# One remainder modulo 256 bytes for every operand of a matrix product: SBUF layout of a hybrid decoder block

## The chip, the cores and the metric

The kernel runs on one core of a Trainium2 chip. The metric is device time in microseconds (us): 2110.35 us is the median of three runs of the kernel before (2109.66 to 2110.6).

## The reference

One decoder block on a sequence of 2048 tokens, width 1024, all in float32. Cut to what matters:

```python
def reference(x, p, w_in, ...):            # x (1, 2048, 1024), p (1, 1, 2048, 256)
    xn = rmsnorm(h, pre_gain)
    z = xn @ w_in                          # (2048, 6152): q, k, v, f logits, g_attn, x_lru, g_lru
    q, k, v, fl, g_attn, x_lru, g_lru = split(z)
    o_attn = forgetting_attention(q, k, v, fl + b_f)      # causal, 8 heads of 128
    y_attn = rmsnorm(o_attn, attn_out_gain) * silu(g_attn)
    xc = causal_depthwise_conv(x_lru, conv_w, conv_b)     # width 4
    o_lru = rg_lru(xc, ...)                # two 128x128 gate products a block, then a scan
    y_lru = rmsnorm(o_lru, lru_out_gain) * silu(g_lru)
    mix = concat([y_attn, y_lru]) @ w_out  # (2048, 2048) @ (2048, 1024)
    h = h + rmsnorm(mix, post_gain)
    e = rmsnorm(p @ w_ple, ple_gain)       # (2048, 256) @ (256, 1024)
    gate = sigmoid(h @ w_ple_gate + b_ple_gate)
    return h + gate * e
```

## The kernel before

Every large product is made of float32r pieces: an operand is split into a high part and the rest (`split`), and `mm3` issues three products (lines 66, 67, 68: high x high, and the two mixed ones) into one PSUM bank. On top of that, the products with `w_in` and `w_out` use seven block products instead of eight (Strassen-Winograd), with sums of blocks formed by VectorE, GpSimd and ScalarE.

The program has three stages in time. **Projections** (to about 1068 us): `z = xn @ w_in`, in two passes over halves of the tokens. Work is divided into units: `v` (v columns and the forget logits, 258 columns wide), `l` (LRU input and gate), `k` (k and q), `g` (attention gate). Every unit has seven block products, `i` = 0 to 6; a unit other than `v` issues 12 products of 128x512 for each `i`, with tokens `XH[i]`, `XL[i]` as the moving operand (512 columns) and a weight block as the stationary one (128x128). For `v` it is the other way round. **Attention** (about 1068 to 1600 us): scores `sbank`, transposes of the probabilities with the identity matrix `ident` (`tbank`), values `obank`. **Output** (to the end): the product with `w_out` (`pbank<-wa,xh` and the like), and the gate product with `w_ple_gate` (`pbank<-wg,h`).

The order of the projections is written out by hand: `plan(slot, phase, f)` puts a step into a calendar of slots (one slot is one block product, 12 matrix products), and the steps are issued slot by slot, in each slot by phase: LOAD, COMBINE, PREP, JOB, MUL, GATE, STORE. All loads and stores of this stage are issued on the SP queue, in calendar order; a load into a tile of a ring waits there until the tile's last user is done, and what follows it on SP waits too. `Ring` computes from the ring's size when a tile comes free.

In the first pass `load_raw` loads a unit's four raw weight quadrants, one to a tile `wf` (ring of 8); `sums`, `high` and `low` make from them the seven operands in tiles `op` (ring of 5: high part in the first half, rest in the second); `keep` stores each to DRAM. In the second pass `fetch` brings the operands back: of nine fetches, five go whole into an `op` tile and four go into two `wf` tiles, one for each part (names `wh`, `wl`).

A tile takes its place in SBUF from its pool's order and size. `wf` tiles have 516 elements (2064 bytes, placed 2080 bytes apart), `op` tiles 2 x 516 (4128 bytes). So operands of one product lie at different remainders modulo 256 bytes. From the built program, remainder modulo 256 of the address at which a partition's data begins:

| tiles | before | after |
|---|---|---|
| `XH`, `XL` of i = 0, 5, 1, 2 | 224 | 224 |
| `XH`, `XL` of i = 3, 4, 6 | 192 | 224 |
| the five `op` slots | 224, 0, 32, 64, 96 | 224 in each |
| `wh`, `wl` (`wf` slots; after: `wr` in `wq` slots) | 224, 0, 32, ... 192 | 224 in each |
| `wph`, `ph` (embedding product) | 192, 64 | 224, 224 |
| LRU gates `xch`, `wgh` | 96, 96 (first pass), 224, 224 | 224, 224 |
| `kh`, `vh` (even, odd heads) | 224, 64 | 224, 224 |
| `qh`, `th`, `tl` | 96 | 224 |
| `ident`; `pr` | 0; 224, 96 | 224; 224, 224 |
| output stage `wa`, `wb`, `xh`, `wg`, `h` | 160, all alike | 224, all alike |

Steps of 512 bytes inside a tile do not change the remainder. In `v` units the moving operand starts at multiples of 1032 bytes, so it has 224, 232, 240 or 248 after.

Of the kernel before, what the change touches and what calls it, by code (L numbers as in the profile page):

```python
# [16 lines left out]
P = 128  # L17
# [15 lines left out]
WS = 2 * WV  # L33
NOP = 5
NOPB = 4
# [36 lines left out]
def hymba_kernel(ctx: ExitStack, tc: tile.TileContext, x, xT, pT, w_p, w_v, w_o, w_ple, w_pg,  # L72
# [27 lines left out]
    ident = const.tile([P, P], F32, name="ident")  # L100
    make_identity(nc, ident)
    onesq = const.tile([P, P], F32, name="onesq")
    nc.gpsimd.memset(onesq, 1.0)
    cmask = const.tile([P, P], F32, name="cmask")
    nc.gpsimd.memset(cmask, 0.0)
    nc.gpsimd.affine_select(out=cmask, in_=cmask, pattern=[[-1, P]], compare_op=ALU.is_ge,
                            fill=-1.0e30, base=0, channel_multiplier=1)
# [13 lines left out]
    rstd_e = const.tile([P, TB], F32, name="rstd_e")  # L121

# [109 lines left out]

    op_ring, wf_ring, ws_ring = Ring(NOP), Ring(8), Ring(2)

    class Unit:
# [17 lines left out]
        def load_raw(self, quad, hf):  # L253
            f = wp.tile([P, WS], F32, name="wf", bufs=8)
            src = w_v[self.n, quad, :, hf * WS:(hf + 1) * WS] if self.v else w_p[self.n, quad]
            nc.sync.dma_start(out=f[:, :self.cols], in_=src)
            self.raw[quad, hf] = f

        def raws(self, hf):
            n = self.cols  # L260
            return [self.raw[q, hf][:, :n] if (q, hf) in self.raw else None for q in range(4)]

        def sums(self, i, hf):
            n = self.cols
            a11, a12, a21, a22 = self.raws(hf)
            sub = lambda o, x, y: nc.gpsimd.tensor_tensor(out=o, in0=x, in1=y, op=ALU.subtract)
            if i == 1 and self.v or i == 2 and not self.v:
                self.S[1, hf] = wp.tile([P, WS], F32, name="ws", bufs=2)[:, :n]
                nc.gpsimd.tensor_tensor(out=self.S[1, hf], in0=a21, in1=a22, op=ALU.add)
            if i == 2:  # L270
                self.S[2, hf] = self.S[1, hf] if self.v else wp.tile([P, WS], F32, name="ws", bufs=2)[:, :n]
# [25 lines left out]
        def fetch(self, i, hf, whole):  # L297
            n = self.cols
            if whole:
                op = wp.tile([P, 2 * WS], F32R, name="op", bufs=NOP)  # L300
                nc.sync.dma_start(out=f32(op[:, :2 * n]), in_=self.stored(i, hf))
                self.ops[i, hf] = op[:, :n], op[:, n:2 * n], op
            else:
                hi = wp.tile([P, WS], F32R, name="wh", tag="wf", bufs=8)
                lo = wp.tile([P, WS], F32R, name="wl", tag="wf", bufs=8)
                nc.sync.dma_start(out=f32(hi[:, :n]), in_=self.stored(i, hf)[:, :n])
                nc.sync.dma_start(out=f32(lo[:, :n]), in_=self.stored(i, hf)[:, n:2 * n])
                self.ops[i, hf] = hi[:, :n], lo[:, :n], None

    def plan_weights(u, lead=4):  # L310

        ends, starts = {}, {}
        halves = range(u.halves)
        quads_of = {0: (0,), 5: (1,), 1: (2, 3), 2: (0, 2, 3), 3: (1,), 4: (0, 2), 6: (3,)}
        for i in u.prep:
            for hf in halves:
                end = u.use(i) + u.halves - 1
                s = max(op_ring.free(), u.use(i) - lead)
                if i == (1 if u.v else 2):
                    s = max(s, ws_ring.ends[-1] + 2 if ws_ring.ends else s)  # L320
                op_ring.take(s, end)
                if u.use(i) - s < 2:
                    print("late operand", u.kind, u.h, i, hf, u.use(i) - s)
                starts[i, hf] = s
                if i in (1, 2, 3, 4):
                    plan(s - 1, PREP, lambda i=i, hf=hf: u.sums(i, hf))
                plan(s, PREP, lambda i=i, hf=hf: u.high(i, hf))
                plan(s + 1, COMBINE, lambda i=i, hf=hf: u.low(i, hf))
                plan(min(s + 2, end), STORE, lambda i=i, hf=hf: u.keep(i, hf))
            if i == 3:  # L330
                ws_ring.take(s, s + 1)
        for quad in (0, 1, 2, 3):
            for hf in halves:
                users = [starts[i, hf] - (i in (1, 2, 3, 4)) for i in u.prep if quad in quads_of[i]]
                last = max(starts[i, hf] + (1 if i in (0, 5, 6) or (i, quad) == (4, 2) else -1)
                           for i in u.prep if quad in quads_of[i])
                s = max(wf_ring.free(), min(users) - lead)
                wf_ring.take(s, last)
                if min(users) - s < 2:
                    print("late raw", u.kind, u.h, quad, hf, min(users) - s)  # L340
                plan(s, LOAD, lambda quad=quad, hf=hf: u.load_raw(quad, hf))
# [3 lines left out]
    def plan_fetch(u):  # L345

        for i in u.order:
            for hf in range(u.halves):
                end = u.use(i) + u.halves - 1
                whole = fetched[0] % (NOP + NOPB) >= NOPB  # L350
                fetched[0] += 1
                ring = op_ring if whole else wf_ring
                s = max(ring.free(), u.use(i) - 7)
                ring.take(s, end)
                if not whole:
                    s = max(s, ring.free())
                    ring.take(s, end)
                if u.use(i) - s < 3:
                    print("late fetch", u.kind, u.h, i, hf, u.use(i) - s)
                plan(s, LOAD, lambda i=i, hf=hf, whole=whole: u.fetch(i, hf, whole))  # L360
# [82 lines left out]
    def plan_v(u, vp):  # L443
# [23 lines left out]
        def combine(i, t):  # L467
            new = {0: "u1", 1: "u5", 5: "o11", 3: "o12"}.get(i)
            if new and t == 0:
                T[new] = vp[0].tile([P, 4, WV], F32, name=names[new], bufs=1)  # L470
# [39 lines left out]
    def plan_job(lw, hb, c, t, new_head):  # L510
# [9 lines left out]
        def s0():  # L520
            J.X = tile_("X", 2, n=515)
# [102 lines left out]
    sg, vp, lw, s = [None], [None], [None, None], {}  # L624
    right = {}

    def open_right(name, cell):
        right[name] = ctx.enter_context(ExitStack())
        cell[0] = pool_(right[name], name, side="right")

# [7 lines left out]
    def square(n, kk, engs):  # L638

        src = s[n, kk // 4][:, kk % 4]  # L640
        eng = engs[kk]
        if (n, eng) not in acc_x:
            acc_x[n, eng] = sg[0].tile([P, 512], F32, name="rx", bufs=2 + len(set(engs)) - 1)
            nc.scalar.activation(acc_x[n, eng], src, AF.Square)
            return
        t = ctile()
        nc.scalar.activation(t, src, AF.Square)

        def accumulate():
            (nc.vector if eng == "dve" else nc.gpsimd).tensor_tensor(out=acc_x[n, eng], in0=acc_x[n, eng], in1=t,  # L650
                                                                     op=ALU.add)
        plan(now[0] + 1, COMBINE, accumulate)

    def column_sums(n):
        accs = [acc_x.pop(k) for k in list(acc_x) if k[0] == n]
        b = er_x[n] = sbank()
        for i in range(4):
            for m, a in enumerate(accs):
                nc.tensor.matmul(b[:, i:i + 1], lhsT=a[:, i * P:(i + 1) * P], rhs=onesq[:, 0:1],
                                 start=m == 0, stop=m == len(accs) - 1)  # L660
# [13 lines left out]
    def spread_scales(n):  # L674
        r_x[n] = sbank()
        nc.tensor.matmul(r_x[n], lhsT=onesq, rhs=dg_x.pop(n), start=True, stop=True)
# [36 lines left out]
    ess = te.tile([P, TB, 2], F32, name="ess", bufs=1)  # L713
# [11 lines left out]
    def ple_weight(j, k):  # L725
        js = slice(j * 512, (j + 1) * 512)
        wf = E["w", j, k] = wp.tile([P, WS], F32, name="wf", bufs=8)[:, :512]
# [20 lines left out]
    def embed_out(tb):  # L748
        b2 = E.pop(("b", tb))
        for j in range(2):  # L750
            js = slice(j * 512, (j + 1) * 512)
            if tb < 4:
                if j == 0:
                    E["v"] = vp[0].tile([P, 4, WV], F32, name=("u1", "u5", "o11", "o12")[tb], bufs=1)
                eo = E["o", tb, j] = E["v"].rearrange("p a b -> p (a b)")[:, js]
# [4 lines left out]
    def embed_sum():  # L760
        nc.vector.tensor_tensor(out=rstd_e, in0=ess[:, :, 0], in1=ess[:, :, 1], op=ALU.add)
# [9 lines left out]
    open_right("sgA", sg)  # L771
# [29 lines left out]
    for n, when in enumerate(((1, 1, 1, 2, 2, 2, 3, 3), (4, 4, 4, 5, 5, 5, 6, 6))):  # L801
        for kk in range(8):
            plan(when[kk], JOB, lambda n=n, kk=kk: square(n, kk, ["dve"] * 8))
# [31 lines left out]
    for _ in range(4):  # L835
        wf_ring.take(-4, -2)
# [64 lines left out]
    plan(130, LOAD, lambda: open_right("sgB", sg))  # L901
    for n in range(2):
# [3 lines left out]
        for kk in range(8):  # L906
            plan(134 + 5 * n + kk // 2, JOB, lambda n=n, kk=kk: square(n, kk, ["dve"] * 8))
# [31 lines left out]
    def bias_tiles():  # L939
        B_.a, B_.b, B_.mg = (vp[0].tile([P, 4, WV], F32, name=x, bufs=1).rearrange("p a b -> p (a b)")  # L940
                             for x in ("u1", "u5", "o11"))
# [120 lines left out]
    def first_mask_adds():  # L1062
        u0.r4 = kvA_[0].tile([P, 4], F32, name="r4", bufs=1)
# [148 lines left out]
    def score_units(h, g, u):  # L1212
# [4 lines left out]
        u.r4 = av.tile([P, 4], F32, name="r4", bufs=4)  # L1217
# [341 lines left out]
    sa = w1.tile([P, TB], F32, name="sa")  # L1559
# [353 lines left out]
```

## Time and profile before

| what | value |
|---|---|
| median of three runs | 2110.35 us (2109.66 to 2110.6) |
| profiled execution: its time, its span | 2115.7 us, 2113.6 us |
| granted TensorE clock | 0.996 |
| TensorE (PE) busy | 2084.5 us, 99% of the span |
| VectorE (DVE), ScalarE (ACT), GpSimd (POOL) busy | 77%, 54%, 33% |
| DMA | 518.91 MB, mean 246 GB/s |

Reading it: PE is the TensorE row; a busy PE does not say that its products run as fast as they can. In groups of instructions ("line engine op, out<-in, shape xcount | busy us, mean ns") the mean of a product counts from its start to its modelled end, and products overlap: the distance from one start to the next is what fills the time. Lines 66, 67 and 68 are the three products of `mm3`; the tile names tell the stage.

### The profile page before, as it was taken

Reading aid. Unit: us, or ns where it says so; the run is one execution under the profiler, and the core shown is the slowest. Engines: PE = TensorE matmul, PEld = TensorE weight load, DVE = VectorE, ACT = ScalarE, POOL = GpSimd, SP = SyncE. Lnnn points to the kernel's source line nnn. Section 1 sums busy time; section 2 is a strip of 40 time slices with the busy share of each in tenths; the row PEclk is TensorE's granted clock in tenths of the full one; section 3 lists DMA queues with packets and bytes.
Section 4 is the critical chain, followed back from the end, with each engine's and each line's share of the span. In section 5 each row is a group of like instructions: output and inputs, shape, how many; then the busy total and the mean of one; then the engine's idle time right before and its main releaser. Section 6 shows DMA issues by size and latency. Waiting matters only on the chain.

```text
span 2113.6 us, 31607 instructions
## 1 busy us (share of the span) xinstructions
PE 2084.5 (99%) x10586; PEld 1743.1 (82%) x10586; DVE 1630.3 (77%) x2706; ACT 1145.6 (54%) x1871; POOL 705.4 (33%) x612
## 2 busy tenths in 40 slices
PE   8899999999999999999999999999999999999999
PEld 6788888888988888888878888888887888888887
DVE  7977988696758877886578888888884778776665
ACT  6435755444337776664267776777674444442232
POOL 3534455332203334733015655566552000000000
PEclk9999999999999999999999999999999999999999
DMA  8598898988888889887757767777653887665553
GB/s 310 204 326 288 296 346 309 341 311 300 286 274 267 281 252 302 267 286 252 267 174 225 231 208 224 232 226 235 200 163 115 278 258 230 194 215 174 180 174 120
DMA packets 274834, 518.91 MB, mean 246 GB/s; under 512 B 27104, under 2 KB 93936, under 8 KB 274672
## 3 DMA queue, kind: packets, MB, share of 16 engines
q1 hardware_dynamic: 274528, 516.86, 74.4%
q8 instruction: 83, 1.36, 0.3%
q14 instruction: 79, 0.65, 0.1%
q10 hardware_dynamic: 144, 0.05, 0.0%
HBM read 314.55 MB, written 202.25 MB: 245 GB/s over the span
## 4 chain that ended last, share of the span: by engine, by line
PE 91%; DVE 4%; DMA 2%; ACT 1%; issue 1%; SPq 0%; POOL 0%; DVEq 0%; ACTq 0%
PE bank L67 15%; PE bank L68 15%; PE bank L66 15%; PE pbank L66 7%; PE pbank L68 7%; PE pbank L67 7%; PE tbank L1261 5%; PE sbank L66 3%; PE sbank L68 3%; PE sbank L67 3%; PE obank L67 3%; PE obank L68 3%; PE obank L66 2%; PE bank L1783 1%; PE tbank L1280 1%
## 5 line engine op out<-in xcount | busy, mean ns | idle before, releaser
L66 PE MATMUL bank<-XH,op 128*128 128x512 f32 x876 | 347.2, 396 | 0.0
L67 PE MATMUL bank<-XL,op 128*128 128x512 f32 x876 | 345.9, 395 | 0.0
L68 PE MATMUL bank<-XH,op 128*128 128x512 f32 x876 | 345.7, 395 | 0.0
L363 DVE TENSOR_TENSOR c<-bank,c 128x512 f32<-128x512 f32 x280 | 186.7, 683 | 125.5 <-PE bank L68 118.1
L58 DVE TENSOR_TENSOR tl<-tbank,th 128x512 fp32r<-128x512 f32 (+1 forms) x320 | 192.2, 607 | 83.9 <-ACT th L52 79.9
L52 ACT ACTIVATE th<-tbank 128x512 fp32r<-128x512 f32 (+1 forms) x320 | 167.6, 530 | 118.2 <-PE tbank L1261 110.4
L68 PEld LDWEIGHTS bank<-XH,op 128*128 128x128 f32 x876 | 164.7, 188 | 39.3
L66 PEld LDWEIGHTS bank<-XH,op 128*128 128x128 f32 x876 | 164.6, 188 | 39.2 <-issue 0.5
L67 PEld LDWEIGHTS bank<-XL,op 128*128 128x128 f32 x876 | 164.7, 188 | 39.1 <-issue 0.5
L1234 ACT ACTIVATE pr<-pr,m 128x640 f32<-128x640 f32 (+7 forms) x124 | 151.9, 1225 | 44.9 <-DVE m L1225 44.5
L1261 PE MATMUL tbank<-ident,pr 128*128 128x128 f32 x1088 | 171.9, 273 | 0.0
L1261 PEld LDWEIGHTS tbank<-ident,pr 128*128 128x128 f32 x1088 | 134.3, 141 | 28.7 <-issue 0.2
L151 POOL TENSOR_TENSOR rsm<-rs,mhalf 128x1 f32<-128x1 f32 x16 | 8.7, 541 | 431.9 <-DVE rs L150 431.9
L66 PE MATMUL sbank<-kh,qh 128*128 128x512 f32 (+3 forms) x320 | 137.3, 429 | 4.2 <-DVE m L1225 2.7
L66 PE MATMUL obank<-th,vh 128*128 128x512 f32 (+1 forms) x320 | 123.5, 386 | 1.3 <-ACT th L52 1.3
L285 ACT ACTIVATE op<-wf 128x512 fp32r<-128x512 f32 (+1 forms) x96 | 60.3, 631 | 116.7 <-PE bank L68 81.7
L67 PE MATMUL obank<-tl,vh 128*128 128x512 f32 (+1 forms) x320 | 118.1, 369 | 1.4 <-DVE tl L58 0.4
L68 PE MATMUL obank<-th,vl 128*128 128x512 f32 (+1 forms) x320 | 117.2, 366 | 0.0
L68 PE MATMUL sbank<-kh,ql 128*128 128x512 f32 (+3 forms) x320 | 116.9, 365 | 0.3 <-DVE ql L1165 0.2
L67 PE MATMUL sbank<-kl,qh 128*128 128x512 f32 (+3 forms) x320 | 116.5, 364 | 0.0
L67 PE MATMUL bank<-op,XH 128*128 128x258 f32 x328 | 93.8, 286 | 4.6 <-DVE op L291 4.6
L68 PE MATMUL bank<-XH,wl 128*128 128x512 f32 x244 | 96.3, 395 | 0.0
(319 smaller groups left out, 5763.6 us busy)
## 6 DMA issues: line engine op xcount, KB each, us to landing
wo_d<-op SPq DMA_DIRECT2D x140, 512.0 KB, 4.6
op<-wo_d SPq DMA_DIRECT2D x79, 512.0 KB, 4.9
wf<-in_w_p_dram SPq DMA_DIRECT2D x80, 256.0 KB, 4.7
wh<-wo_d SPq DMA_DIRECT2D x61, 256.0 KB, 3.9
wl<-wo_d SPq DMA_DIRECT2D x61, 256.0 KB, 4.3
vo_d<-op SPq DMA_DIRECT2D x28, 516.0 KB, 3.4
wst<-wt_d SPq DMA_DIRECT2D x56, 256.0 KB, 3.5
wst<-in_w_o_dram SPq DMA_DIRECT2D x40, 256.0 KB, 3.2
```

Source lines behind the costliest of these rows:

```text
L52: nc.scalar.activation(hi, src, AF.Copy)
L58: eng.tensor_tensor(out=lo, in0=src, in1=f32(hi), op=ALU.subtract)
L66: nc.tensor.matmul(out, lhsT=wh, rhs=xh, start=start, stop=False)
L67: nc.tensor.matmul(out, lhsT=wh, rhs=xl, start=False, stop=False)
L68: nc.tensor.matmul(out, lhsT=wl, rhs=xh, start=False, stop=stop)
L151: nc.gpsimd.tensor_tensor(out=o, in0=t, in1=mhalf[:, :n], op=ALU.pow)
L285: nc.scalar.activation(op[:, :n], self.source(i, hf), AF.Copy)
L363: nc.vector.tensor_tensor(out=o, in0=x, in1=y, op=ALU.add)
L1234: nc.scalar.activation(pr[0][:, :L], pr[0][:, :L], AF.Exp, bias=m2, scale=-1.0, accum_out=u.r4[:, i:i + 1])
L1261: nc.tensor.transpose(b[:, i * P:(i + 1) * P], u.P[i][:, sb * P:(sb + 1) * P], ident)
L1280: nc.tensor.transpose(b[:, i * P:(i + 1) * P], u.r4[:, i:i + 1].broadcast_to([P, P]), ident)
L1783: nc.tensor.transpose(b[:, k * P:(k + 1) * P], u.xt[:, kk * P:(kk + 1) * P], ident)
```

## The change

All operands of matrix products are put at one remainder modulo 256 bytes. For that, tiles are padded (`WT` = 1088 elements, 4352 bytes, for `op` and the new raw tile; `ws` has half of it), small constants move ahead of the large ones, `onesq` moves from the constants into a pool that is opened twice, `rx` accumulators become `ws` or `v` tiles, and some small tiles (`r4`, `ess`, `sa`, `X`) change size. The raw weights are loaded two quadrants to a tile `wq` (ring of 4) by one transfer; the host packs them accordingly. A fetch of the second pass is always one transfer of both parts into one tile. Tile `X` of the LRU jobs has one buffer instead of two in the second pass (pool `lw1`). The counts and the order of instructions on PE, VectorE and ScalarE are the same as before.

```diff
+WT = 1088
-NOPB = 4
+NRAW = 4
...
-    op_ring, wf_ring, ws_ring = Ring(NOP), Ring(8), Ring(2)
+    op_ring, wq_ring, ws_ring = Ring(NOP), Ring(NRAW), Ring(2)
...
-        def load_raw(self, quad, hf):
-            f = wp.tile([P, WS], F32, name="wf", bufs=8)
-            src = w_v[self.n, quad, :, hf * WS:(hf + 1) * WS] if self.v else w_p[self.n, quad]
-            nc.sync.dma_start(out=f[:, :self.cols], in_=src)
-            self.raw[quad, hf] = f
+        def load_raw(self, n):
+            f = wp.tile([P, WT], F32, name="wq", bufs=NRAW)
+            m = 2 * self.cols
+            nc.sync.dma_start(out=f[:, :m], in_=(w_v if self.v else w_p)[self.n, n])
+            for i in range(2):
+                self.raw[(n, i) if self.v else (n + 2 * i, 0)] = f[:, i * self.cols:(i + 1) * self.cols]
...
-            op = wp.tile([P, 2 * WS], F32R, name="op", bufs=NOP)
+            op = wp.tile([P, WT], F32R, name="op", bufs=NOP)
...
-        def fetch(self, i, hf, whole):
+        def fetch(self, i, hf, own):
             n = self.cols
-            if whole:
-                op = wp.tile([P, 2 * WS], F32R, name="op", bufs=NOP)
-                nc.sync.dma_start(out=f32(op[:, :2 * n]), in_=self.stored(i, hf))
-                self.ops[i, hf] = op[:, :n], op[:, n:2 * n], op
-            else:
-                hi = wp.tile([P, WS], F32R, name="wh", tag="wf", bufs=8)
-                lo = wp.tile([P, WS], F32R, name="wl", tag="wf", bufs=8)
-                nc.sync.dma_start(out=f32(hi[:, :n]), in_=self.stored(i, hf)[:, :n])
-                nc.sync.dma_start(out=f32(lo[:, :n]), in_=self.stored(i, hf)[:, n:2 * n])
-                self.ops[i, hf] = hi[:, :n], lo[:, :n], None
+            op = (wp.tile([P, WT], F32R, name="op", bufs=NOP) if own else
+                  wp.tile([P, WT], F32R, name="wr", tag="wq", bufs=NRAW))
+            nc.sync.dma_start(out=f32(op[:, :2 * n]), in_=self.stored(i, hf))
+            self.ops[i, hf] = op[:, :n], op[:, n:2 * n], op
...
-        for quad in (0, 1, 2, 3):
-            for hf in halves:
...
-                s = max(wf_ring.free(), min(users) - lead)
-                wf_ring.take(s, last)
+        for n in range(4 if u.v else 2):
+            quads = (n,) if u.v else (n, n + 2)
...
+            s = max(wq_ring.free(), min(users) - lead)
+            wq_ring.take(s, max(ends_))
...
-            J.X = tile_("X", 2, n=515)
+            J.X = tile_("X", lw[2], n=576)[:, :515]
...
+    def open_stage(name):
+        open_right(name, sg)
+        sg[1] = sg[0].tile([P, P], F32, name="onesq", bufs=1)
+        nc.gpsimd.memset(sg[1], 1.0)
...
     def open_lw(name):
         open_right(name, lw)
+        lw[2] = 2 if name == "lw0" else 1
...
-        u0.r4 = kvA_[0].tile([P, 4], F32, name="r4", bufs=1)
+        u0.r4 = kvA_[0].tile([P, 32], F32, name="r4", bufs=1)[:, :4]
```

What moves is on the queues. The first place is the SP queue in the first pass, around the loads of one `l` unit (`wf` and `wq` are raw weights, `wo_d<-op` the stores of `keep`, `xr_d` and `gl_d` results of units, `X`, `G` and `yl_d` the LRU jobs). Before:

```order
L295 DMA wo_d<-op 128x1024 x2
L403 DMA xr_d<-c 128x512
L621 DMA yl_d<-G 128x512
L295 DMA wo_d<-op 128x1024
L256 DMA wf<-in_w_p_dram 128x512
L295 DMA wo_d<-op 128x1024 x2
L256 DMA wf<-in_w_p_dram 128x512 x3
L587 DMA G<-gl_d 128x512
```

And now:

```order
L294 DMA wo_d<-op 128x1024 x2
L397 DMA xr_d<-c 128x512
L615 DMA yl_d<-G 128x512
L294 DMA wo_d<-op 128x1024
L255 DMA wq<-in_w_p_dram 128x1024 x2
L294 DMA wo_d<-op 128x1024 x2
L581 DMA G<-gl_d 128x512
```

Three of the four quadrants, which stood behind two more stores, now stand ahead of them; four transfers became two of twice the size. By the ring's own count a unit's later quadrants were loaded two slots ahead of their first user, and now all are loaded four or more ahead (in the first `l` unit two and three, for the last quadrants of the second `v` unit two).

The second place is the SP queue in the second pass (`op`, `wh`, `wl`, `wr` are fetched operands, `c<-in_w_gates_dram` the LRU gate weights). Before:

```order
L301 DMA op<-wo_d 128x1024
L306 DMA wh<-wo_d 128x512
L307 DMA wl<-wo_d 128x512
L306 DMA wh<-wo_d 128x512
L307 DMA wl<-wo_d 128x512
L522 DMA X<-xr_d 128x515
L525 DMA c<-in_w_gates_dram 128x256
L306 DMA wh<-wo_d 128x512
L307 DMA wl<-wo_d 128x512
```

And now:

```order
L300 DMA op<-wo_d 128x1024
L300 DMA wr<-wo_d 128x1024 x2
L516 DMA X<-xr_d 128x515
L519 DMA c<-in_w_gates_dram 128x256
L300 DMA wr<-wo_d 128x1024
```

The order of the fetches is the same, a pair of transfers is one now, and the load of `X` stands where it stood; but with one buffer it waits for VectorE's last convolution step on the tile's previous content, and the loads behind it wait with it.

On GpSimd the three short memsets (`mhalf`, `two`, `one`) come ahead of `ident`, `onesq` and `cmask`, and `onesq` is set a second time before the second token half.

More of the change, by code (lines that the diff above doesn't have):

```diff
@@ L121, in hymba_kernel @@
     rstd_e = const.tile([P, TB], F32, name="rstd_e")
+    ident = const.tile([P, P], F32, name="ident")
+    make_identity(nc, ident)
+    cmask = const.tile([P, P], F32, name="cmask")
+    nc.gpsimd.memset(cmask, 0.0)
+    nc.gpsimd.affine_select(out=cmask, in_=cmask, pattern=[[-1, P]], compare_op=ALU.is_ge,
+                            fill=-1.0e30, base=0, channel_multiplier=1)
     def log1p_exp_neg_abs(o, a, pool, n):
@@ L349, in plan_fetch @@
                 end = u.use(i) + u.halves - 1
-                whole = fetched[0] % (NOP + NOPB) >= NOPB
+                own = fetched[0] % (NOP + NRAW) >= NRAW
                 fetched[0] += 1
-                ring = op_ring if whole else wf_ring
+                ring = op_ring if own else wq_ring
                 s = max(ring.free(), u.use(i) - 7)
                 ring.take(s, end)
-                if not whole:
-                    s = max(s, ring.free())
-                    ring.take(s, end)
                 if u.use(i) - s < 3:
                     print("late fetch", u.kind, u.h, i, hf, u.use(i) - s)
-                plan(s, LOAD, lambda i=i, hf=hf, whole=whole: u.fetch(i, hf, whole))
+                plan(s, LOAD, lambda i=i, hf=hf, own=own: u.fetch(i, hf, own))
     def add(o, x, y):
@@ L469, in combine @@
             if new and t == 0:
-                T[new] = vp[0].tile([P, 4, WV], F32, name=names[new], bufs=1)
+                T[new] = v_tile(names[new]).rearrange("p (a b) -> p a b", b=WV)
             q = B.pop((i, t))
@@ L636, in hymba_kernel, with square @@
     acc_x, r_x, er_x, dg_x = {}, {}, {}, {}
-    def square(n, kk, engs):
+    def square(p, n, kk):
         src = s[n, kk // 4][:, kk % 4]
[L641 to L644, printed above, removed]
+        if kk == 0:
+            acc_x[n] = (v_tile(("u1", "o11")[n]) if p else wp.tile([P, WT // 2], F32, name="ws", bufs=2))[:, :512]
+            nc.scalar.activation(acc_x[n], src, AF.Square)
             return
@@ L647, in square @@
         nc.scalar.activation(t, src, AF.Square)
[L649 to L652, printed above, removed]
+        plan(now[0] + 1, COMBINE, lambda: add(acc_x[n], acc_x[n], t))
     def column_sums(n):
-        accs = [acc_x.pop(k) for k in list(acc_x) if k[0] == n]
-        b = er_x[n] = sbank()
+        a, b = acc_x.pop(n), sbank()
+        er_x[n] = b
         for i in range(4):
-            for m, a in enumerate(accs):
-                nc.tensor.matmul(b[:, i:i + 1], lhsT=a[:, i * P:(i + 1) * P], rhs=onesq[:, 0:1],
-                                 start=m == 0, stop=m == len(accs) - 1)
+            nc.tensor.matmul(b[:, i:i + 1], lhsT=a[:, i * P:(i + 1) * P], rhs=sg[1][:, 0:1], start=True, stop=True)
     def column_roots(p, n):
@@ L675, in spread_scales @@
         r_x[n] = sbank()
-        nc.tensor.matmul(r_x[n], lhsT=onesq, rhs=dg_x.pop(n), start=True, stop=True)
+        nc.tensor.matmul(r_x[n], lhsT=sg[1], rhs=dg_x.pop(n), start=True, stop=True)
     def normalize(n, kk):
@@ L834, in hymba_kernel @@
                + [Unit("k", n, 1, KB + 7 * n) for n in range(8)] + [Unit("g", n, 1, GB + 7 * n) for n in range(4)])
-    for _ in range(4):
-        wf_ring.take(-4, -2)
+    for _ in range(2):
+        wq_ring.take(-4, -2)
     for u in units_A:
@@ L1558, in hymba_kernel @@
     now[:] = -99, 0
-    sa = w1.tile([P, TB], F32, name="sa")
+    sa = w1.tile([P, 4 * TB], F32, name="sa")
     G_ = Ctx()
@@ L1861, in quads @@
     def quads(ca, cb, m):
-        return [wk[:, 4 * kh:4 * kh + 4, col:col + m].reshape(P, 4 * m) for col in (ca, cb) for kh in range(2)]
+        return [np.concatenate([wk[:, 4 * kh:4 * kh + 4, col:col + m].reshape(P, 4 * m) for col in (ca, cb)], axis=1)
+                for kh in range(2)]
     pairs = [quads(1024 + h * P, h * P, P) for h in range(NH)]
```

60 lines of the change are left out of this document (29 added, 31 removed).

## Prediction

> **What bounds the kernel now.** I read the busy times first, then the chain that ended last, then the waits of PE, then the groups of PE.
>
> ```profile
> PE 2084.5 (99%) x10586; PEld 1743.1 (82%) x10586; DVE 1630.3 (77%) x2706; ACT 1145.6 (54%) x1871; POOL 705.4 (33%) x612
> ...
> PE 91%; DVE 4%; DMA 2%; ACT 1%; issue 1%; SPq 0%; POOL 0%; DVEq 0%; ACTq 0%
> ```
>
> PE is busy 99% of the span and makes 91% of the chain. Its longest waits are small:
>
> ```profile
> PE bank L66 <- ACT wph L52: 5.8, 1, 5.8
> PE bank L67 <- DVE op L291: 4.6, 3, 1.9
> ```
>
> The first is the start-up; the list's twelve entries add up to 22 us. So time can come only from the products themselves, or be lost by new waits. The groups of 128x512 products, which all do the same amount of work, differ:
>
> ```profile
> L66 PE MATMUL bank<-XH,op 128*128 128x512 f32 x876 | 347.2, 396 | 0.0
> L67 PE MATMUL bank<-XL,op 128*128 128x512 f32 x876 | 345.9, 395 | 0.0
> L68 PE MATMUL bank<-XH,op 128*128 128x512 f32 x876 | 345.7, 395 | 0.0
> ...
> L68 PE MATMUL bank<-XH,wl 128*128 128x512 f32 x244 | 96.3, 395 | 0.0
> L67 PE MATMUL bank<-XL,wh 128*128 128x512 f32 x244 | 96.2, 394 | 0.0
> L66 PE MATMUL bank<-XH,wh 128*128 128x512 f32 x244 | 96.0, 393 | 0.0
> ...
> L66 PE MATMUL pbank<-wb,xh 128*128 128x512 f32 x224 | 87.4, 390 | 0.0
> L68 PE MATMUL pbank<-wb,xl 128*128 128x512 f32 x224 | 87.2, 389 | 0.0
> L67 PE MATMUL pbank<-wb,xh 128*128 128x512 f32 x224 | 87.1, 389 | 0.0
> ```
>
> The 3360 products of the units take 1327.3 us, 395.0 ns each; the 672 of the output stage, whose operands all lie at remainder 160, take 261.7 us, 389.4 ns. That could be the stage and not the address. The timeline of PE decides, where one `op` slot (remainder 224, that of `XH`) follows another slot within the same unit, some microseconds apart, and, last, the output stage:
>
> ```profile
> 196.63 0.39 PE L66 MATMUL bank<-XH,op 128*128 128x512 f32 x1
> ...
> 200.59 0.40 PE L68 MATMUL bank<-XH,op 128*128 128x512 f32 x1
> ...
> 202.19 0.39 PE L66 MATMUL bank<-XH,op 128*128 128x512 f32 x1
> ...
> 204.68 0.40 PE L68 MATMUL bank<-XH,op 128*128 128x512 f32 x1
> ...
> 1679.66 0.39 PE L66 MATMUL pbank<-wb,xh 128*128 128x512 f32 x1
> ...
> 1684.88 0.39 PE L68 MATMUL pbank<-wb,xl 128*128 128x512 f32 x1
> ```
>
> From start to start: 17 products from 196.63 to 200.59 us at unlike remainders, 233 ns each; 11 from 202.19 to 204.68 at equal ones, 226.4 ns; 23 of the output stage, 227.0 ns. (A mean of 395 ns in the groups goes with 233 from start to start, 389 with 227: the difference of 162 is the overlap.) Unit, stage and shape are the same in the first two, and only the slot's address differs. Where moving and stationary operand agree modulo 256, a product costs about 6 ns less.
>
> Must they agree modulo 512? After the change `op` slots alternate between 224 and 480 modulo 512, so it matters. In one unit `XH` lies at 480 modulo 512, `wh` at 224 (equal modulo 256), `wl` at 192:
>
> ```profile
> L67 PE MATMUL bank<-XL,wh 128*128 128x512 f32 x5 | 2.0, 396 | 0.0
> ...
> L66 PE MATMUL bank<-XH,wh 128*128 128x512 f32 x5 | 1.9, 390 | 0.0
> ```
>
> (Groups of PE from 643.6 to 646.6 us.) The first `XH,wh` of each three runs while the next weights come again from `wh`, and it has the good time, 390; `XL,wh` runs while `wl` is loaded, and has 396. So a product is slowed by the weights loaded under it, and 256 suffices here.
>
> **A rule against the change.** The Trainium skill, "TensorE: Matmul & The Clock Gate", part 2 (step by step), has PE read the moving operand and the weights through two independent ports, so that loading the next weights takes nothing from the running product; "SBUF — State Buffer", "Who interferes with whom", adds that PE never waits on anyone. By that the sum would be 0, and the time 2110 us; the 233 against 226.4 ns above disagree.
>
> **The sum**, in the profiled execution.
>
> 1. *Unit products.* 3360 x (395.0 - 389.4) = 18.8 us. All lies on PE's path. The bounds: against the plain 389 ns it is 20.2; if half of the operands did not profit, 9.4. I take 18.8.
>
> 2. *LRU gate products.* They stand between unit products and already agree (96, 96), but in sixes among unlike ones:
>
> ```profile
> L68 PE MATMUL sbank<-xch,wgl 128*128 128x512 f32 x64 | 25.2, 393 | 0.0
> ...
> L66 PE MATMUL sbank<-xch,wgh 128*128 128x512 f32 x64 | 25.1, 392 | 0.0
> ```
>
> Six in a row are too few to settle. The three groups (the one between has 25.1 us) make 75.4 us for 192, or 392.7 ns; with equal neighbours each loses 3.3 ns, 0.6 us in all (0 to 0.7).
>
> 3. *Attention.* Groups of PE from 1068 to 1600 us:
>
> ```profile
> L67 PE MATMUL obank<-tl,vh 128*128 128x512 f32 x214 | 84.8, 396 | 0.2 <-DVE tl L58 0.2
> L68 PE MATMUL obank<-th,vl 128*128 128x512 f32 x214 | 84.6, 395 | 0.0
> L68 PE MATMUL sbank<-kh,ql 128*128 128x512 f32 x200 | 79.8, 399 | 0.3 <-DVE ql L1165 0.2
> L67 PE MATMUL sbank<-kl,qh 128*128 128x512 f32 x200 | 79.5, 397 | 0.0
> ```
>
> Full gain: 214 x (6.6 + 5.6) + 200 x (9.6 + 7.6) ns = 6.0 us. But products come in threes and sixes between transposes, and after these it takes some to settle. The nearest rows are products with equal remainders that stand between transposes:
>
> ```profile
> 1595.89 0.40 PE L67 MATMUL bank<-wa,xh 128*128 128x512 f32 x1
> ...
> 1596.58 0.39 PE L67 MATMUL bank<-wa,xh 128*128 128x512 f32 x1
> ...
> 1597.03 0.39 PE L66 MATMUL obank<-th,vh 128*128 128x512 f32 x1
> ```
>
> The first product of this six is hidden in the end of the transposes; the next three, from 1595.89 to 1596.58, take 230 ns each, all five to 1597.03 us 228. So threes would have half of the gain and sixes somewhat more, if settling stays as it is; `ident` now agrees too, which may spare it. I take 2.5 us, between 0 and 6.0.
>
> 4. *Transposes.* Before, their remainders are unlike; an unlike 128x128 could not be seen to cost anything:
>
> ```profile
> L1261 PE MATMUL tbank<-ident,pr 128*128 128x128 f32 x1050 | 165.9, 273 | 0.0
> L1280 PE MATMUL tbank<-ident,r 128*128 128x128 f32 x128 | 19.3, 273 | 0.5 <-DVE r L1469 0.5
> ```
>
> `pr` is read row by row, `r` repeats one column, and both take 273 ns. I take 0. If the 6 ns had the other sign here, 1178 x 6 ns = 7 us would be lost; that is a bound, and no row asks for it.
>
> 5. *258 columns.* Groups of `v` products and of 256 columns at equal remainders:
>
> ```profile
> L66 PE MATMUL bank<-op,XH 128*128 128x258 f32 x328 | 93.6, 285 | 0.0
> L67 PE MATMUL pbank<-wg,h 128*128 128x256 f32 x12 | 3.4, 283 | 0.0
> ```
>
> Two columns more account for about 1 ns of the 2. 1344 x up to 1 ns: I take 0, -1 to +1 us.
>
> 6. *Embedding products* (`wph`, 192 of 128x512, 64 to 192): full gain 192 x 6 ns = 1.2 us, but start-up is held by VectorE in part. 0.5. *Gate products and their transposes in the output stage*: remainders equal before, `ident` excepted; settling after 32 groups of transposes, 0.5 (0 to 1.9).
>
> 7. *Raw loads, two to a tile.* They stand earlier on SP than before, so GpSimd's sums wait less; PE waits for nothing of them. 0.
>
> 8. *One buffer for X.* SP now waits at each of the 23 later loads of the second pass. What is behind: fetches, stores, `G`. The hold, from the timelines of SP, DVE and ACT for one job (last, the row of the page for `X`, with its time to landing):
>
> ```profile
> 708.88 0.38 SPq L522 DMA_DIRECT2D X<-xr_d  x1
> ...
> 713.17 0.75 DVE L532 SCALAR_TENSOR_TENSOR XC<-X,hv,XC 128x512 f32<-128x512 f32 x1
> ...
> 721.58 0.81 ACT L529 ACTIVATE XC<-X,hv 128x512 f32<-128x512 f32 x1 [2.94 <-DVE I L569]
> ...
> X<-xr_d SPq DMA_DIRECT2D x32, 257.5 KB, 5.5
> ```
>
> The DVE row is the last convolution step of the job before, which ends at 713.9 us. So SP would be held from 708.9 to 713.9 us, 5 us. The cover is the fetch's lead, from the rows of tile `wh` between 585 and 614 us:
>
> ```profile
> L66 PE MATMUL bank<-XH,wh x6: 388/390/392, 610.3 to 613.7; 128*128 128x512 f32 x6
> ...
> L306 SPq DMA_DIRECT2D wh<-wo_d x5: 319/320/620, 588.0 to 613.0; - x5
> ```
>
> Issued at 588.0, used at 610.3; even if it takes as long to land as `X` does, 17 us are free, and 5 are taken. `X` itself was used 12.7 us after its issue (`XC` at 721.58); with 5 us of hold and 5.5 to land it still comes in time, by 2 us, and it is ScalarE, not PE, that would wait. 0; without that cover, the rival below.
>
> 9. *Memsets, `onesq`, padding*: nothing on the path waits for them. 0.
>
> Sum: 18.8 + 0.6 + 2.5 + 0.5 + 0.5 = 22.9 us. The profiled execution took 2115.7 us; less 22.9 that is 2092.8, or 1.08% less. On the median of 2110.35 us: 2087.5 us.
>
> **The rivals.**
>
> *The change does not do what it says*: the weights loaded under a product take nothing from it, and the differences in the trace come from neighbours and stages. Then nothing is gained, 2110 us. For it: the LRU gates agree and have 393 ns. Against it: the same unit at 233 and 226.4 ns, and `XH,wh` at 390 beside `XL,wh` at 396. Chance 7%. This is what the two pages of the Trainium skill named above would have.
>
> *It takes 512, or the good state lasts only part of the time.* Then about half of item 1 and little of item 3: 9.4 + 1.6 = 11 us, 2099 us. For it: `XL,wh` and `XH,wl` never settled; against it: `XH,wh` at 390. Chance 8%.
>
> *One buffer for X decides*, slower: SP stands behind VectorE so long that fetched operands come late. It decides from a hold of 17 us on. Beyond that each of 23 jobs stops PE for what is over: from 18 us the gain is eaten up (23 x 1 us), and at 18.2 us 23 x 1.2 = 28 us are lost, 2087.5 + 28 = 2115 us. For it: VectorE is busy 77% and behind its plan by 5 us already. Against it: 12 us of margin. Chance 5%.
>
> **How the numbers follow.** The forecast (all of item 1, attention in part) has 80%. Its own range: with every item at its best (20.2 + 0.7 + 6.0 + 1.2 + 1.9 + 1 = 31) 2079; with item 3 at 0, item 4 at -7 and item 5 at -1, 2098. The ends together are unlikely; I take 2080 at the low end, and 2099 at the high end so that the half case is in. Outside stay 7% and 5% and some rest. What a measurement can tell from no change is 0.2%, 4 us: the forecast and the half case are faster, 88%; the first rival is the same, 7%; the third is slower, 5%.
>
> **What the profile after would show.** Item 1: the mean of `bank<-XH,op` at 389 to 390, starts 226 to 227 ns apart, in every unit, and the same for the `wr` fetches. Item 3: `obank<-tl,vh` and `sbank<-kh,ql` between 389 and 396. Item 4: `tbank<-ident,pr` still 273. Item 8: waits on SP before `X`, none on PE for `wr` or `op`. The busy time of DVE and ACT unchanged, their shares higher. I am wrong if the mean stays at 395 (first rival), if only some slots of `op` go to 389 (second), or if PE shows waits on DMA between 590 and 960 us (third).

## The result, and the profile after

The changed kernel took 2093.92 us (median of four runs, 2091.41 to 2095.91), the kernel before 2110.01 us beside it (four runs, 2107.76 to 2110.6). The ratio is 0.9925, interval 0.9908 to 0.9942: faster by 16.1 us, or 0.75%, and the interval leaves out 1. The forecast was 2087.5 us with a range from 2080 to 2099. Thirteen runs of the changed kernel, in three sets, have the median 2092.8 us (2089.51 to 2095.91).

The profiled execution took 2091.41 us, its span is 2089.6 us. Its page, the busy times and the chain that ended last:

```profile
PE 2062.3 (99%) x10586; PEld 1744.5 (83%) x10586; DVE 1625.5 (78%) x2706; ACT 1143.7 (55%) x1871; POOL 705.5 (34%) x613
...
PE 92%; DVE 4%; DMA 2%; ACT 1%; issue 1%; SPq 0%; DVEq 0%; ACTq 0%
```

PE still fills the span, with the same 10586 products, and its busy time fell by 22.2 us; DVE and ACT kept theirs within 5 us. The groups of PE (lines 67, 68, 69 are now the three products of `mm3`):

```profile
L67 PE MATMUL bank<-XH,op 128*128 128x512 f32 x876 | 342.3, 391 | 0.0
L69 PE MATMUL bank<-XH,op 128*128 128x512 f32 x876 | 340.9, 389 | 0.0
L68 PE MATMUL bank<-XL,op 128*128 128x512 f32 x876 | 340.8, 389 | 0.0
...
L69 PE MATMUL bank<-op,XL 128*128 128x258 f32 x328 | 95.9, 292 | 0.0
...
L67 PE MATMUL bank<-XH,wr 128*128 128x512 f32 x244 | 94.9, 389 | 0.0
...
L68 PE MATMUL bank<-op,XH 128*128 128x258 f32 x328 | 94.9, 289 | 2.8 <-DVE op L290 2.8
L67 PE MATMUL bank<-op,XH 128*128 128x258 f32 x328 | 94.7, 289 | 0.0
```

The unit products went from 393 to 396 ns to 389 to 391, `op` and `wr` alike. The `v` products (258 columns) went the other way: 285 to 286 ns before, 289 to 292 now. From start to start the unit products stand 226.8 ns apart; 22 products in the first pass, timeline of PE:

```profile
203.68 0.39 PE L68 MATMUL bank<-XL,op 128*128 128x512 f32 x1
...
208.67 0.39 PE L69 MATMUL bank<-XH,op 128*128 128x512 f32 x1
```

Where the 16 us come from is seen from two points that every profile has: the start of the first and of the last unit product of the projections. Timeline of PE, first the kernel before, then the changed kernel:

```profile
112.83 0.39 PE L66 MATMUL bank<-XH,op 128*128 128x512 f32 x1
...
1067.20 0.39 PE L68 MATMUL bank<-XH,op 128*128 128x512 f32 x1
```

```profile
108.90 0.40 PE L67 MATMUL bank<-XH,op 128*128 128x512 f32 x1
...
1046.08 0.39 PE L69 MATMUL bank<-XH,op 128*128 128x512 f32 x1
```

That stretch took 954.4 us and takes 937.2 us now, 17.2 us less. To split it, I summed from the trace's start times, for each kind of product, the time from each start to the next:

| us from start to start | before | after | op128 | op4 | v96 |
|---|---|---|---|---|---|
| 3360 unit products | 782.8 | 763.3 | 782.3 | 782.2 | 763.3 |
| 192 LRU gate products | 44.2 | 43.6 | 43.9 | 44.1 | 43.6 |
| 1008 `v` products (without the first unit) | 121.4 | 124.3 | 121.2 | 121.2 | 120.2 |
| the whole stretch | 954.4 | 937.2 | 953.3 | 953.4 | 933.0 |

(The three right columns are experiments below.) -19.5, -0.6 and +2.9 make the -17.2. The output stage, from its first product to the last one, took 515.5 us before and 515.3 after.

The attention stage, from the last unit product to the first of the output stage, took 525.9 us in the one profile of before and between 521.1 and 524.2 in all later profiles. The start-up before the first unit product took 112.8 us, and then between 108.9 and 111.2. These two scatter by 2 to 3 us among kernels that have the same code there, so a difference of 2 to 4 us to one profile of before can't be put down to the change. The profiled execution of before was also 5.7 us above the median of 2110.01 us, and that of the changed kernel 2.5 us below its own; that is why the two profiles differ by 24.3 us and the medians by 16.1.

### The profile page after: what moved, and what is told of

Same layout as the page of the kernel before. It is cut to its first block, busy times and chain, and to the rows that moved or that the text cites. A ratio compares the mean times of both kernels' runs of the same rounds, so it can differ in the third digit from the quotient of the medians.

```text
span 2089.6 us, 31351 instructions
## 1 busy us (share of the span) xinstructions
PE 2062.3 (99%) x10586; PEld 1744.5 (83%) x10586; DVE 1625.5 (78%) x2706; ACT 1143.7 (55%) x1871; POOL 705.5 (34%) x613
## 4 chain that ended last, share of the span: by engine, by line
PE 92%; DVE 4%; DMA 2%; ACT 1%; issue 1%; SPq 0%; DVEq 0%; ACTq 0%
PE bank L69 15%; PE bank L67 15%; PE bank L68 15%; PE pbank L69 7%; PE pbank L67 7%; PE pbank L68 7%; PE tbank L1258 5%; PE sbank L67 3%; PE sbank L69 3%; PE sbank L68 3%; PE obank L68 3%; PE obank L69 3%; PE obank L67 3%; DVE pr L1222 1%; PE bank L1780 1%
## 5 line engine op out<-in xcount | busy, mean ns | idle before, releaser
L67 PE MATMUL bank<-XH,op 128*128 128x512 f32 x876 | 342.3, 391 | 0.0
L69 PE MATMUL bank<-XH,op 128*128 128x512 f32 x876 | 340.9, 389 | 0.0
L68 PE MATMUL bank<-XL,op 128*128 128x512 f32 x876 | 340.8, 389 | 0.0
L1258 PE MATMUL tbank<-ident,pr 128*128 128x128 f32 x1088 | 171.9, 273 | 0.0
L67 PE MATMUL obank<-th,vh 128*128 128x512 f32 (+1 forms) x320 | 123.2, 385 | 0.8 <-ACT th L53 0.8
L284 ACT ACTIVATE op<-wq 128x512 fp32r<-128x512 f32 (+1 forms) x96 | 60.0, 629 | 110.5 <-PE bank L69 73.0
L69 PE MATMUL bank<-op,XL 128*128 128x258 f32 x328 | 95.9, 292 | 0.0
```

The source lines that it names most:

```text
L67: nc.tensor.matmul(out, lhsT=wh, rhs=xh, start=start, stop=False)
L68: nc.tensor.matmul(out, lhsT=wh, rhs=xl, start=False, stop=False)
L69: nc.tensor.matmul(out, lhsT=wl, rhs=xh, start=False, stop=stop)
L1258: nc.tensor.transpose(b[:, i * P:(i + 1) * P], u.P[i][:, sb * P:(sb + 1) * P], ident)
```

## The experiments

**The same kernel again.**

> The changed kernel once more, beside the kernel before on the same chip, to separate the effect from what differs between executions. Theory A (address): the effect is in every execution, 20 us on the unit products alone (3360 products, from 233 to 227 ns apart), so the ratio is 0.990 to 0.992. Rival (part of the profiled pair's 24 us was start-up and clock of those two executions): the ratio is 0.992 to 0.994 and the unit products still show 389 ns.

It took 2091.2 us, ratio 0.9914 (0.99 to 0.9928) to 2109.52 us before. The stretch was 937.2 us again, unit products 763.3 us: the projections repeat to a tenth, the rest scatters. This ratio lies in theory A's range, and that of the first four runs, 0.9925, in the rival's. The rival is right in so far as 24 us of the profiled pair were more than the effect; the 19.5 us of the unit products are in every execution that was profiled.

**Only the remainder undone.** The tiles, transfers, queues and single `X` buffer of the changed kernel stay; the operands of all units but `v` start 128 bytes further inside their padded tiles.

```diff
-            op = wp.tile([P, WT], F32R, name="op", bufs=NOP)
+            op = wp.tile([P, WT], F32R, name="op", bufs=NOP)[:, (0 if self.v else 32):]
...
-                  wp.tile([P, WT], F32R, name="wr", tag="wq", bufs=NRAW))
+                  wp.tile([P, WT], F32R, name="wr", tag="wq", bufs=NRAW))[:, (0 if self.v else 32):]
```

> The changed kernel with the operands of all units but v shifted by 128 bytes inside their padded tiles (slices start at element 32), nothing else moved: same transfers, same tiles, same order. Theory A (the remainder sets the time under which the next weights are loaded): unit products go back to 395 ns in the groups and 232 to 233 ns apart, 18 to 20 us more than the changed kernel, 2110 to 2114 us. Rival B (the gain is from fewer and larger transfers, or from where the tiles lie in SBUF as such): unit products stay at 389 ns and the time within 3 us of the changed kernel.

It took 2110.37 us, ratio 1.0005 (0.9997 to 1.0014). Its groups of PE, and the two marks of the stretch:

```profile
L67 PE MATMUL bank<-XH,op 128*128 128x512 f32 x876 | 347.0, 396 | 0.0
L68 PE MATMUL bank<-XL,op 128*128 128x512 f32 x876 | 345.6, 395 | 0.0
L69 PE MATMUL bank<-XH,op 128*128 128x512 f32 x876 | 345.6, 395 | 0.0
```

```profile
109.45 0.40 PE L67 MATMUL bank<-XH,op 128*128 128x512 f32 x1
...
1062.79 0.40 PE L69 MATMUL bank<-XH,op 128*128 128x512 f32 x1
```

All three groups are back at 395 to 396 ns and the stretch at 953.3 us. Nothing differs from the changed kernel but 32 elements of offset, and the granted clock was 0.998 in both profiles. So the address remainder makes the gain, and what else the change does adds up to nothing that the time shows (2110.37 us here, 2109.52 us before beside it).

The weight loads themselves are no longer than in the changed kernel. Their row on PEld, the changed kernel first, then op128:

```profile
L67 PEld LDWEIGHTS bank<-XH,op 128*128 128x128 f32 x876 | 164.5, 188 | 34.0 <-issue 0.5
```

```profile
L67 PEld LDWEIGHTS bank<-XH,op 128*128 128x128 f32 x876 | 165.0, 188 | 38.5 <-issue 0.5
```

A load takes 188 ns in both; only the products, under which the loads run, stand further apart.

**How equal must it be?** The same edit with an offset of one element, 4 bytes:

```diff
-            op = wp.tile([P, WT], F32R, name="op", bufs=NOP)
+            op = wp.tile([P, WT], F32R, name="op", bufs=NOP)[:, (0 if self.v else 1):]
```

(and the same for `wr`).

> Operand tiles of all units but v are shifted by one element: remainder 228 against 224 of XH and XL; everything else as in the changed kernel. Theory (exact remainder): the product is fast only where the remainders are equal to the byte; then all unit products go back to 232 to 233 ns from start to start, some 782 us in all, and the time is about 2110 us. Rival (blocks of 32 or 64 bytes): it is enough that both addresses lie in the same block of 32 bytes modulo 256; then nothing changes, 226.8 ns, 763 us, 2091 us. Second rival (near misses cost most, as in the v units, where an offset of 0 to 24 bytes goes with up to 137 ns against 119): above 233 ns and above 2110 us.

It took 2108.58 us, ratio 0.9992 (0.9983 to 1.0002). 18 products on the timeline of PE:

```profile
203.64 0.39 PE L69 MATMUL bank<-XH,op 128*128 128x512 f32 x1
...
207.82 0.39 PE L69 MATMUL bank<-XH,op 128*128 128x512 f32 x1
```

They are 232.2 ns apart, as with 128 bytes. One element of difference already loses all of it. The rivals fail: there is no block of 32 bytes inside which it is enough, and a near miss costs 512-column products no more than a far one.

**The `v` operands alone, 96 bytes away.** In the changed kernel the moving operand of a `v` product is 0, 8, 16 or 24 bytes from the stationary one modulo 256.

```diff
-            op = wp.tile([P, WT], F32R, name="op", bufs=NOP)
+            op = wp.tile([P, WT], F32R, name="op", bufs=NOP)[:, (24 if self.v else 0):]
```

(and the same for `wr`).

> The changed kernel with only the operands of the v units shifted by 96 bytes, so that the 258-column products have unlike remainders again (moving 64 to 88, weights 224). In the profile after, these products repeat a fixed pattern of 120, 123, 137, 130, 119, 118 ns by their offset, 124.5 on average, against 120.4 before. Theory A (like remainders help only where moving and weights agree exactly, and the near misses of 8 to 24 bytes cost): 1344 x 4 = 3 to 5 us less than the changed kernel, groups of 258 columns back to 283 to 285 ns. Rival (258 columns cost the same at any remainder, and the rise in the profile after is chance): same time, groups stay at 285 to 292 ns.

It took 2087.86 us, ratio 0.9897 (0.9884 to 0.9911). The groups of `v` products and the marks of the stretch:

```profile
L68 PE MATMUL bank<-op,XH 128*128 128x258 f32 x328 | 93.7, 286 | 3.8 <-DVE op L290 3.8
L67 PE MATMUL bank<-op,XH 128*128 128x258 f32 x328 | 93.7, 286 | 0.0
L69 PE MATMUL bank<-op,XL 128*128 128x258 f32 x328 | 92.4, 282 | 0.0
```

```profile
108.96 0.39 PE L67 MATMUL bank<-XH,op 128*128 128x512 f32 x1
...
1042.00 0.39 PE L69 MATMUL bank<-XH,op 128*128 128x512 f32 x1
```

The groups are at 282 to 286 ns, within 1 ns of the 283 to 285 expected. The stretch is 933.0 us, 4.1 less than in the changed kernel, and the `v` products account for all of it (124.3 to 120.2 us). The time is 3.3 us below the 2091.2 us of the changed kernel beside it. Once more, with the changed kernel beside it:

> Only the operands of the v units are shifted by 96 bytes, once more, to see whether the 3 us of the first run stand. Theory (a distance of 0 to 24 bytes lets the v products fall into a slow state, a distance of 96 to 120 never does): every v unit at 119 ns, v products 166 to 167 us in all, and the time 3 to 5 us below the changed kernel of this call. Rival (the first run's 3 us were scatter of the executions): within 1 us of the changed kernel.

> The changed kernel again, as the neighbour of the two others of this call. All theories: 2090 to 2094 us; the v products stand in two states, 124 ns and 119 ns from start to start at the same addresses, with the same units in each state as in the two earlier profiles.

2087.82 us against 2094.12; ratios 0.9894 (0.988 to 0.9907) and 0.9918 (0.9905 to 0.9932). The difference of 6.3 us is more than the 3 to 5 expected; all 1344 `v` products took 166.4 us from start to start, as expected. Over both sets the eight runs with the shift have the median 2087.87 us, 4.9 us below the changed kernel's 2092.8. This is the fastest version that was run.

The `v` products of the changed kernel do not all suffer. After the first unit each group of them stands in one of two states for its whole length. From start to start, without waits, the groups of one profile in their order (672, 24, 120, 120, 72 products) have 124.4, 123.2, 118.9, 124.2 and 118.9 ns, the same in six profiles with equal unit remainders and unshifted `v` operands (the changed kernel's three, and attn128, ident0 and split below). In op128 and op4, whose `v` operands have the same addresses, they have 118.9, 118.8, 124.2, 118.9 and 124.1 (124.0 in op128): every group is in the other state. The fourth group, groups of PE between 775 and 789 us of the changed kernel, and then between 788 and 802 us of op4:

```profile
L69 PE MATMUL bank<-op,XL 128*128 128x258 f32 x36 | 10.5, 291 | 0.0
L67 PE MATMUL bank<-op,XH 128*128 128x258 f32 x36 | 10.3, 287 | 0.0
L68 PE MATMUL bank<-op,XH 128*128 128x258 f32 x36 | 10.3, 286 | 0.0
```

```profile
L67 PE MATMUL bank<-op,XH 128*128 128x258 f32 x36 | 10.2, 283 | 0.0
L68 PE MATMUL bank<-op,XH 128*128 128x258 f32 x36 | 10.1, 281 | 0.0
L69 PE MATMUL bank<-op,XL 128*128 128x258 f32 x36 | 10.0, 279 | 0.0
```

The same products at the same addresses, 287 ns against 281. So these addresses alone do not set the state. Nor does the order of PE's instructions: the first `v` unit, which comes ahead of all other unit products and is broken up by waits of PE, has 123.6 to 124.2 ns in the mean in the changed kernel's three profiles, but in ident0, at the same addresses, most of it has 119 and only the last 36 products have 124. What sets the state stays open.

That the group of 672 products came to stand 124 ns apart in the changed kernel is therefore not the price of the small distance alone, and for the prediction it is bad luck: in op128 and op4, at the same distances, it stands 118.9 ns apart, and the `v` products of the stretch took 121.2 us, against 121.4 in the kernel before. With 96 bytes of distance no group has 124 ns; all have 119.

**Is 96 particular?** The same edit with 32 elements, 128 bytes:

> Only the operands of the v units (258 columns) are shifted, by 128 bytes (96 in an earlier run). Theory (near miss): in the changed kernel the moving operand of v products is 0, 8, 16 or 24 bytes from the stationary one modulo 256, and small distances cost these products 4 to 6 ns each; any distance well away from 0 gives the old time; then v products sum to 166 to 169 us and the time is about 2088 us. Rival (the gain at 96 bytes is particular to that distance): v products sum to 169 to 172 us, and 2090 to 2091 us.

It took 2091.03 us (2087.54 to 2094.72), ratio 0.9909 (0.9892 to 0.9926). All groups after the first unit have 120.6 to 121.0 ns, with no second state, and the stretch is 934.5 us, 2.7 less than in the changed kernel. All 1344 `v` products took 169.4 us from start to start, against 168.8 in the kernel before and 166.4 at 96 bytes. So the theory is right that the 124 ns go and that the old time comes back; but its 166 to 169 us and 2088 us were missed, and both measured numbers are the rival's (169 to 172 us, 2090 to 2091 us): 96 bytes gain 1.6 ns a product that 128 bytes do not. The time alone can't tell this run from the changed kernel.

**The attention operands alone undone.** Tiles `qh`, `ql`, `th` and `tl` are shifted by 128 bytes.

```diff
-            u.qh = ap.tile([P, 512], F32R, name="qh", bufs=2)
+            u.qh = ap.tile([P, 576], F32R, name="qh", bufs=2)[:, 32:544]
...
-        th = av.tile([P, 512], F32R, name="th", bufs=THB)
+        th = av.tile([P, 576], F32R, name="th", bufs=THB)[:, 32:544]
```

(`ql` and `tl` alike.)

> Only the attention stage is undone: qh, ql, th and tl are shifted by 128 bytes (remainder 96 against 224 of kh, kl, vh and vl), all else as in the changed kernel. Theory (most of the attention products never settle between transposes, so the equal remainders gave about 2 us): from start to start obank products of 512 columns sum to 163 to 164 us and sbank to 160 to 161, against 162.5 and 159.2 to 159.7; the time is 1.5 to 3 us above the changed kernel in this call. Rival (attention products gained their full 6 ns, the stage before was slowed by something else): 5 to 6 us above. Second rival (attention gains nothing from the remainder): equal to the changed kernel within 0.5 us.

It took 2091.79 us, ratio 0.9915 (0.9902 to 0.9929), no more than its neighbour's 2094.12. Its groups, then those of the neighbour:

```profile
L68 PE MATMUL obank<-tl,vh 128*128 128x512 f32 x224 | 88.6, 396 | 0.0
L69 PE MATMUL obank<-th,vl 128*128 128x512 f32 x224 | 88.3, 394 | 0.0
L69 PE MATMUL sbank<-kh,ql 128*128 128x512 f32 x200 | 79.7, 398 | 0.1
L68 PE MATMUL sbank<-kl,qh 128*128 128x512 f32 x200 | 79.4, 397 | 0.0
```

```profile
L68 PE MATMUL obank<-tl,vh 128*128 128x512 f32 x224 | 88.3, 394 | 0.0
L69 PE MATMUL obank<-th,vl 128*128 128x512 f32 x224 | 88.1, 394 | 0.0
L69 PE MATMUL sbank<-kh,ql 128*128 128x512 f32 x200 | 79.5, 397 | 0.1
L68 PE MATMUL sbank<-kl,qh 128*128 128x512 f32 x200 | 78.9, 394 | 0.0
```

The four groups differ by 0.3 + 0.2 + 0.2 + 0.5 = 1.2 us. From start to start, the measure of the expectation, `obank` products sum to 163.0 us, at the theory's lower bound, and `sbank` products to 159.3, no more than in the changed kernel (162.4 to 162.6 and 159.2 to 160.0). In the one profile of before they were 163.8 and 160.7, so the two sums fell by about 2 us with the change, of which undoing the addresses gives back less than 1 us; the rest is not explained. The stage took 522.6 us, inside the 521.1 to 524.2 of the kernels that have equal remainders there. So the addresses are worth about 1 us at most to the attention's products, and in time less than the 3 us by which the stage scatters. That is below the theory's 1.5 to 3 us; the full gain of the first rival is excluded, and no gain at all, the second rival, is not excluded by the time.

**The identity matrix at another remainder.** `ident` moves ahead of two small constants, and so from remainder 224 to 0:

```diff
+    ident = const.tile([P, P], F32, name="ident")
+    make_identity(nc, ident)
...
-    ident = const.tile([P, P], F32, name="ident")
-    make_identity(nc, ident)
```

> The identity matrix stands at remainder 0 instead of 224, all else as in the changed kernel. Theory: a transpose of 128 columns is not slowed by unlike remainders, and products that follow transposes settle as slowly with an equal identity as with an unlike one; then 2091 us, transposes about 101 us from start to start, obank and sbank products 231 to 236 ns apart. Rival: the equal identity is what gave the attention stage its 2.3 us; then about 2093.5 us, all of the loss between 1050 and 1590 us.

It took 2093.27 us, ratio 0.9922 (0.9903 to 0.9941). That is the rival's number, but also only 0.5 us above the median of the changed kernel's thirteen runs, which reach from 2089.51 to 2095.91, so the time decides nothing. The attention stage took 524.2 us, as it did in one of the changed kernel's three profiles. The transposes:

```profile
L1258 PE MATMUL tbank<-ident,pr 128*128 128x128 f32 x1088 | 171.9, 273 | 0.0
```

That is the row of the changed kernel to the digit (1088 of 171.9 us, 273 ns); from start to start they take 101.4 us against 100.0 to 101.8 in its three profiles, and `obank` and `sbank` products 162.7 and 160.2 us against 162.4 to 162.6 and 159.2 to 160.0. So no cost of an unlike identity is seen, neither in the transposes nor in the products that follow them.

**The merged transfers split again**, raw weights and fetches:

```diff
-            nc.sync.dma_start(out=f[:, :m], in_=(w_v if self.v else w_p)[self.n, n])
...
+                c = slice(i * self.cols, (i + 1) * self.cols)
+                nc.sync.dma_start(out=f[:, c], in_=(w_v if self.v else w_p)[self.n, n][:, c])
...
-            nc.sync.dma_start(out=f32(op[:, :2 * n]), in_=self.stored(i, hf))
+            for c in (slice(0, 2 * n),) if own else (slice(0, n), slice(n, 2 * n)):
+                nc.sync.dma_start(out=f32(op[:, c]), in_=self.stored(i, hf)[:, c])
```

> The changed kernel with its merged transfers split again: two transfers for each raw weight tile and two for each fetch into a raw slot, into the same tiles at the same addresses. Theory A (all gain is from the addresses): same time as the changed kernel within 2 us, unit products at 389 ns. Rival B (fewer and larger transfers give part of the gain): slower by 3 us or more, with waits on transfers at PE, GpSimd or ScalarE.

It took 2090.55 us, ratio 0.9912 (0.9899 to 0.9926). One of its groups:

```profile
L67 PE MATMUL bank<-XH,op 128*128 128x512 f32 x876 | 342.2, 391 | 0.0
```

Unit products took 763.3 us from start to start and the stretch 937.2, both as in the changed kernel. Merging is worth nothing here.

## Why the prediction was right in its main step and 5 to 6 us too low

- *Unit products, 18.8 us.* Shown. The trace gives 782.8 - 763.3 = 19.5 us, and op128, where only the offset is undone, gives 19.0 of them back. The reading of one and the same unit at 233 and 226.4 ns carried over to all units. The prediction also read, from five products, that what counts are the weights loaded under a product. Over all unit products of the kernel before, with their addresses from the built program, both pairs count. 80 products agree with their own weights and not with those loaded under them, and stand 233.7 ns from the next; 80 are the other way round, 231.5 ns; 315 agree with both, 228.1 ns; the rest agree with neither, 233.1 ns. The Trainium skill, "TensorE: Matmul & The Clock Gate", part 2 (step by step), would have the weight loads take nothing from the running product, by two independent read ports; op128 disagrees, 395 against 389 ns and 2110.37 against 2091.2 us.
- *256 or 512.* `op` slots alternate between 224 and 480 modulo 512 while `XH` stays, and the groups of `op` are at 389 to 391 ns as a whole, `wr` at 389. By the addresses of the built program, 1613 products that agree modulo 512 as well stand 226.8 ns apart, and so do 1523 whose weights lie 256 bytes off modulo 512. The half case is excluded, 256 it is.
- *258 columns, 0 (-1 to +1).* This step failed. I took equal remainders from the 256-column products of the output stage as the nearest row (283 ns) and concluded that a nearly equal one costs nothing. In fact the `v` products came to lie 0 to 24 bytes off, where a state of 124 ns was seen beside one of 119, and 2.9 us were lost in the stretch; 96 bytes of distance gives them back and 1.2 us more. That the loss came to so much is luck, as op128 and op4 show; that the term could be a loss at all is what the prediction had no row for.
- *Attention, 2.5 us.* That the stage gets only part of the full gain was right, the size was not: about 1 us in the products, by the run that undoes it. From the row of six (230, then 228 ns) I gave threes half the gain; in the changed kernel the `obank` products of 512 columns stand 231 ns apart in the median, against 232 before. Of the two rows named ahead, `obank<-tl,vh` came to 394 ns, and `sbank<-kh,ql` to 398, above the 389 to 396 forecast. Why products between transposes gain so little is argued (they have no time to settle) and not shown.
- *LRU gates, 0.6 us*: 0.6 (44.2 to 43.6). *Output gate, 0.5 us*: 0.2. *Embedding, 0.5 us*: its products take 56.2 us before and between 52.5 and 54.8 in the kernels after; with one profile of before, and a start-up that scatters by 2 us, this can't be settled. *Transposes, 0*: 273 ns still.
- *One buffer for X, 0.* As predicted. What the load of `X` waited for on SP (us in total, times, longest), and the rows of tile `X` on SP between 580 and 960 us:

```profile
SPq L516 <- DVE XC L526: 74.0, 21, 5.5
```

```profile
L516 SPq DMA_DIRECT2D X<-xr_d x23: 319/320/376, 591.3 to 927.7; - x23
...
  ACT XC L523: 5.8, 1
```

  21 holds of 3.5 us in the mean and 5.5 at the longest, against 5 forecast and 17 of cover. ScalarE waited for a late `X` once, 5.8 us, as it did in the kernel before (once, 4.7 us); PE never sat idle before a product that reads `wr`, and it has no wait listed between 590 and 960 us. The slower rival had its hold, but not its price.

The measured terms, 19.5 + 0.6 + 1 + 0.2 - 2.9 = 18.4 us, against 22.9 forecast and 17.0 between the medians (2109.8 of all 41 runs of before, 2092.8 of 13): the 258 columns make 2.9 us of the miss, the attention 1.5. What lies between 18.4 and 17.0 is inside the scatter of the start-up and the attention stage.

## What to carry to other kernels

When PE is busy all the time, compare groups of products that do equal work, and look at the addresses where they differ: here an SBUF offset alone, with no instruction changed, was worth 0.9%. Undo such a change by an offset inside a padded tile, since that touches no queue and no order. And read the rows of operands that come near to equal without being equal: the 258-column products could come to 124 ns instead of 119 there, which cost 3 us in the changed kernel and nothing in two of its neighbours.

## What was not expected of the hardware

- Equal means equal: an offset of 4 bytes costs a 512-column product as much as one of 128 (232.4 ns in the mean of unit products in both, against 226.8).
- The 258-column products have, at the same addresses 0 to 24 bytes off, two lasting states, 118.9 and 124.2 ns, and neither these addresses nor the order of PE's instructions selects between them; at 96 bytes they have 119.0, at 128 bytes 120.6.
- Agreement has to hold for a product's own weights and for those loaded under it; a product with only one of the two is not fast (233.7 and 231.5 ns, against 228.1 with both, in the kernel before). Why it costs less when the addresses agree modulo 256 is not shown by any run here; the weight load itself takes 188 ns either way.
